# Two weight sums of a projection group on GpSimd, a fourth raw weight buffer there, and stores of x spread over an FFN's start

## The chip, the core and the metric

The kernel runs on one core of a Trainium2 chip. Five engines work side by side on their own queues: TensorE (PE; its weight loads are listed as PEld), VectorE (DVE), ScalarE (ACT), GpSimd (POOL) and SyncE (SP, which here only issues DMAs). Data lies in SBUF (128 partitions); matmul results lie in PSUM banks. The metric is the device time of one execution in microseconds. The kernel before takes 2344.84 us, the median of 3 runs (2342.85 to 2346.62).

## The reference

Two layers of an encoder trunk on 512 tokens of width 1024, all in float32. Each layer is: a half-step SwiGLU FFN, a mixer, a second half-step FFN, each with an RMSNorm before and after.

```python
for l in range(DEPTH):
    y = swiglu(rmsnorm(h, ffn1_pre_g[l]), ffn1_w_gu[l], ffn1_w_down[l])
    h = h + 0.5 * rmsnorm(y, ffn1_post_g[l])
    u = rmsnorm(h, mix_pre_g[l])
    proj = u @ w_in[l]
    qa, ka, va, qb, kb, vb, qc, kc, vc, gl = jnp.split(proj, split_at, axis=-1)
    ...  # neighbourhood, sliding-window and differential attention, gates, w_out
    h = h + rmsnorm(merged @ w_out[l], mix_post_g[l])
    y = swiglu(rmsnorm(h, ffn2_pre_g[l]), ffn2_w_gu[l], ffn2_w_down[l])
    h = h + 0.5 * rmsnorm(y, ffn2_post_g[l])
```

The change lies in `proj = u @ w_in[l]` of both layers and in the start of the first FFN.

## The kernel before

**Precision.** TensorE multiplies in a reduced float32 form. Every operand is therefore split into a high part (a rounding copy by ScalarE) and a low part (the raw value minus the high part, by DVE), and a product is three matmuls: high x high, high x low, low x high.

**Seven products.** Most of `w_in` and of the FFN's gate and up weights goes through `class Seven`: two column blocks of weights by the two halves of the inner dimension, times four quadrants of the activations, are computed as seven products in place of eight (a Strassen-like scheme). One such pair of column blocks is a *group*: 84 matmuls of 256 columns, line 687. A group needs two raw weight tiles of 128x1024 (512 KB each), which hold four 128x512 quarters, and sums of these quarters. For group g:

- `fetches` (L614) issues the two raw loads from SP's queue, into a pool `wr` of three buffers that rotate.
- `sum13` (L628, DVE, 128x1024) makes two sums into a tile r; `high1`, `low1` (L632, L637) split the first raw tile; `high13`, `low13` (L642, L647) split r.
- `sum2` (L651, DVE, 128x512) adds half of r and a quarter of the first raw tile into the second raw tile, in place.
- `high12`, `low12` (L657, L661) split a quarter of the second raw tile; `sum4` (L665, DVE, 128x512) then overwrites that quarter with its sum with the other one; `high24`, `low24` (L669, L674) split the whole second raw tile.

The four weight sums of a group are thus the two in `sum13`, `sum2` and `sum4`. The first raw tile is free after `low1` and `sum2`, the second after `low24`.

The products p1 to p7 of a group run while the weights of the next are prepared. ScalarE copies between banks (L726, L731, L735), DVE adds (`add21` L740, `add22` L745), and when `add22` is done a bank is free for a later group's first product.

**The projection** (`project`) has 13 groups a layer. What a group yields is evicted by ScalarE (L1396, L1400), split again (L1412, L1413), for queries and keys rotated (L1459 to L1461) or, for values, transposed by TensorE (L1434) and evicted (L1440, L1441), and stored to DRAM for the mixer: `store` (L1407) issues these DMAs from GpSimd's queue. The tiles for all this come from 16 buffers of the tag `t` (128x512 each). Beside its DMAs, GpSimd computes almost nothing in the kernel: some fills at the start and one-element copies (`mark`, L287) that pace DMAs in the FFNs.

**The order** of the instructions on each engine is not as written: a scheduler of the building layer sorts them, and each engine then executes its list strictly in order, each instruction waiting for its semaphores. A pool decides at build time which buffer a tile gets.

**The first FFN's start.** x comes in transposed; `keep` (L906 to L911) transposes it back, by TensorE into the one bank `o` (L908), copies it by ScalarE into a tile `h` (L910; from four buffers of the tag `t` that `finish` also uses, L853 to L856) and stores it to DRAM in two halves per token block, from SP's queue (L911). There are four token blocks, eight copies and eight stores of 256 KB. They stand in a list `later`, from which two entries are taken at each weight tile of the dense products that come before the first group.

Of the kernel before, what the change touches and what calls it, by code (L numbers as in the profile page):

```python
# [10 lines left out]
F32 = mybir.dt.float32  # L11
F32R = mybir.dt.float32r
AF = mybir.ActivationFunctionType
ALU = mybir.AluOpType
AX = mybir.AxisListType

P = 128
# [4 lines left out]
NT = T // P  # L22
FF = 2816
KF = FF // P
# [4 lines left out]
WB = 8  # L29
# [85 lines left out]
def encoder_kernel(ctx: ExitStack, tc: tile.TileContext, order, xT, wts, cols, rows, rpb, consts, tables, out):  # L115
# [9 lines left out]
    BUFS = {"X": 6, "n": 2, "wr": 3, "wp": 2, "wq": 2}  # L125
    WP = BUFS["wp"] + BUFS["wq"]
    SKEW = 80
    ABUFS = {"f": {"t": 4, "x": 10}, "p": {"t": 16, "x": 10, "rr": 2}, "m": {"t": 5, "h": 4, "rr": 2, "tx": 5, "st": 14, "gd": 2, "g": 10, "s": 2, "pt": 4}}
    PBUFS = {"mm": 2, "mx": 2, "at": 3, "o": 1}

    def open_phase(kind):
# [10 lines left out]
    def nm(s):  # L142
        serial[0] += 1
        return f"{s}{serial[0]}"
# [53 lines left out]
    def holder(tag):  # L198
        return lambda: [big(tag, F32R, (P, HB, P), name="w") for _ in range(2)]

    def fetch(parts, eng=None):
        raw = sb.tile([P, WB, P], F32, tag="wr", name=nm("wr"), bufs=BUFS["wr"])
        src = wts[len(stream["raw"])].rearrange("p (a b) -> p a b", b=P)
        for c in range(0, WB, WB // parts):
            cs = slice(c, c + WB // parts)
            (eng or stream["eng"]).dma_start(raw[:, cs, :], src[:, cs, :])
        stream["raw"].append(raw)
# [167 lines left out]
    class Squares:  # L375
        def __init__(self):
            self.acc, self.seen = None, []
# [203 lines left out]
    class Seven:  # L581


        def __init__(self, z, count):
            self.z, self.count = z, count
            self.hi, self.lo, self.raw = {}, {}, {}
            self.raws, self.W = {}, {}
            self.groups = [{} for _ in range(count)]
            self.seeds = None
# [24 lines left out]
        def fetches(self, g):  # L614
            if g < self.count:
                self.W[g] = {}
                for _ in range(2):
                    fetch(1, nc.sync)
                self.raws[g] = [t.rearrange("p (a b) c -> p a b c", a=2) for t in stream["raw"][-2:]]

        def wpair(self, name):
# [26 lines left out]

        def sum2(self, g):
            r = self.raws[g]  # L650
            V.tensor_tensor(out=r[1][:, 1], in0=self.W[g]["r13"][:, 1], in1=r[0][:, 0], op=ALU.add)  # L651

        def high12(self, g):
            w = self.W[g]
# [7 lines left out]

        def sum4(self, g):
            r = self.raws[g][1]
            V.tensor_tensor(out=r[:, 0], in0=r[:, 0], in1=r[:, 1], op=ALU.add)  # L665

        def high24(self, g):
            self.W[g]["h24"] = self.wpair("h24")
# [96 lines left out]
    def ffn(l, which, X, accs):  # L765
# [93 lines left out]
                V.scalar_tensor_tensor(out=place(m), in0=pu, scalar=-1.0, in1=t, op0=ALU.mult, op1=ALU.mult)  # L859


        S = Seven(z, KF - plain)
        hi, lo, raw, groups, count = S.hi, S.lo, S.raw, S.groups, S.count
        divide, less, quadrants = S.divide, S.less, S.quadrants
        later = stream["later"]
# [4 lines left out]
        def at(fn, *args):  # L870
            return lambda: fn(*args)
# [13 lines left out]
        if first:  # L885
            s = Squares()
            for hs in HALVES:
                for b in range(KD):
                    s.add(V, hT[:, b, hs], hs)
            rB = pair("rB", F32)[:, 0, :]  # L890
            u1 = dense1(gu, l, KF + 1, X.blocks, tag="at", midway=lambda: finish_rms(s, rB))
            prepare(rowt)
            n = [sb.tile([P, 2, HK, HT], F32, tag="n", name=nm("n"), bufs=BUFS["n"]) for _ in range(2)]
            own = [sb.tile([P, 2, HK, HT], F32R, tag="X", name=nm("X"), bufs=BUFS["X"]) for _ in range(2)]
            quadrants(n)

            def normal(b):
                V.scalar_tensor_tensor(
                    out=n[b // HK][:, :, b % HK, :], in0=two(hT[:, b, :]), scalar=gcol(b), in1=two(rB),
                    op0=ALU.mult, op1=ALU.mult,  # L900
                )

            def keep(tb):
                d = dr.tile([P, D], F32, tag="kept", name=nm("kept"), bufs=2 * NT)
                for i in range(2):
                    tp = bank("o")  # L906
                    for k in range(HB):
                        PE.transpose(tp[:, k * P : (k + 1) * P], hT[:, HB * i + k, tb * P : (tb + 1) * P], ident)  # L908
                    t = big("t", name="h")
                    A.activation(t, tp, AF.Copy)  # L910
                    nc.sync.dma_start(d[:, i * T : (i + 1) * T], t)  # L911
                kept.append(d)

            stream["pace"] = 2
            for b in range(0, KD, 2):
                later.append(some(at(normal, b), at(normal, b + 1)))
            later.append(at(divide, "11", own[0][:, 0], own[1][:, 0]))
            later.append(at(divide, "22", own[0][:, 1], own[1][:, 1]))
            later.extend(at(keep, tb) for tb in range(NT))
            later.append(at(gap, "gaph", 48))  # L920
        else:
            quadrants(X.raw)
            for i, j in ((0, 0), (1, 0), (1, 1)):
                k = f"{i + 1}{j + 1}"
                hi[k], lo[k] = X.hi[i][:, j], X.lo[i][:, j]
# [11 lines left out]
                at(S.low1, 0),  # L937
            )
        )
        if not first:  # L940
            u1 = dense1(gu, l, KF + 1, X.blocks, tag="at")
        finish(0, g0, u0)
# [427 lines left out]
    def project(l, op, accs):  # L1370
# [115 lines left out]
            now()  # L1486

        made = {}
        S = Seven(z, len(GROUPS))
        count, groups, later = S.count, S.groups, stream["later"]  # L1490

        def some(*calls):
# [2 lines left out]
        def at(fn, *args):  # L1495
            return lambda: fn(*args)
# [661 lines left out]
```

## Time and profile before

| what | us |
|---|---|
| median of 3 runs | 2344.84 (2342.85 to 2346.62) |
| profiled execution, its own time | 2345.54 |
| its span, first to last instruction | 2343.7 |
| PE busy | 2329.0 (99%) |
| DVE busy | 1917.7 (82%) |
| ACT busy | 1455.2 (62%) |
| POOL busy | 235.7 (10%) |
| mean granted TensorE clock | 0.999 of full speed |

Rows of a timeline give the start in us from the span's start, the duration in us, the engine, the source line, the operation, `out<-in` by the program's names and the shapes; in square brackets stands the engine's idle time before the instruction, and what ended it. Rows of groups give the busy time, the mean duration in ns, and the idle time before. A duration is longer than the distance to the next instruction's start where an engine overlaps the end of one with the start of the next, so that distance (the pitch) is what an instruction costs on a full engine.

### The profile page before, as it was taken

The numbers are of one execution on the slowest core, as the hardware profiler recorded it, in microseconds if no ns is written. First come the engines' busy times: TensorE is split into PE (matmuls) and PEld (weight loads), VectorE is DVE, ScalarE is ACT, GpSimd is POOL, SyncE is SP. The second block draws the span as 40 slices with busy tenths as digits, with TensorE's granted clock in tenths as the row PEclk, the third lists the DMA queues.
The fourth block names the chain that finished last, engine by engine and source line by source line (L and its number), as shares of the span: only waits on it lengthen the run. The fifth ranks groups of instructions, "written<-read, shape, count | busy, mean of one in ns | idle before, by whom it ended". The sixth has DMA issues, their size and how long they took to land.

```text
span 2343.7 us, 40580 instructions
## 1 busy us (share of the span) xinstructions
PE 2329.0 (99%) x15278; PEld 2104.4 (90%) x15278; DVE 1917.7 (82%) x3103; ACT 1455.2 (62%) x2734; POOL 235.7 (10%) x378
## 2 busy tenths in 40 slices
PE   9999999999999999999999999999999999999998
PEld 7999889998888889998899998899988888999987
DVE  8987988868987778888888878798689776888796
ACT  6565566668766465655665555666687764656563
POOL 0111001110122001110001100011102110011100
PEclk9999999999999999999999999999999999999999
DMA  5566446668556425665536565276775664356642
GB/s 190 148 172 194 147 150 194 200 218 241 150 179 214 149 96 151 168 160 161 171 103 165 166 171 197 92 219 197 231 221 147 187 207 142 97 162 171 180 142 92
DMA packets 135636, 395.18 MB, mean 169 GB/s; under 512 B 19216, under 2 KB 23952, under 8 KB 134928
## 3 DMA queue, kind: packets, MB, share of 16 engines
q1 hardware_dynamic: 99712, 260.11, 35.8%
q0 software_dynamic: 22080, 84.95, 13.3%
q10 hardware_dynamic: 13648, 47.53, 6.6%
q8 instruction: 120, 1.97, 0.4%
q14 instruction: 76, 0.62, 0.1%
HBM read 326.98 MB, written 80.74 MB: 174 GB/s over the span
## 4 chain that ended last, share of the span: by engine, by line
PE 88%; DMA 4%; DVE 3%; issue 2%; ACT 1%; SPq 0%; POOL 0%; ACTq 0%; DVEq 0%; POOLq 0%
PE mm L687 20%; PE mx L687 10%; PE mm L1155 8%; PE mm L323 6%; PE mm L322 6%; PE mm L324 6%; PE mx L1155 5%; PE at L687 5%; PE at L1155 5%; DMA wr<-in_wts_dram 2%; PE at L322 2%; PE at L323 2%; PE at L324 2%; PE o L1155 1%; PE mx L1677 1%
## 5 line engine op out<-in xcount | busy, mean ns | idle before, releaser
L687 PE MATMUL mm<-X,h 128*128 128x256 f32 x1600 | 285.5, 278 | 2.3 <-DVE v L745 2.2
L687 PEld LDWEIGHTS mm<-X,h 128*128 128x128 f32 x1600 | 243.1, 188 | 4.3 <-DVE v L745 3.4
L687 PE MATMUL mm<-ht,h 128*128 128x256 f32 x800 | 224.0, 280 | 1.0 <-ACT at L726 1.0
L687 PE MATMUL mm<-ht,l 128*128 128x256 f32 x800 | 223.6, 279 | 0.0
L687 PE MATMUL mm<-lt,h 128*128 128x256 f32 x800 | 222.8, 278 | 0.0
L687 PE MATMUL mx<-ht,h 128*128 128x256 f32 x800 | 221.6, 277 | 0.4 <-ACT v L731 0.2
L687 PE MATMUL mm<-X,l 128*128 128x256 f32 x800 | 221.5, 277 | 0.0
L687 PE MATMUL mx<-ht,l 128*128 128x256 f32 x800 | 221.2, 276 | 0.0
L687 PE MATMUL mx<-lt,h 128*128 128x256 f32 x800 | 221.2, 276 | 0.0
L219 ACT ACTIVATE w<-wr 128x512 fp32r<-128x512 f32 x240 | 148.1, 626 | 96.4 <-PE mm L324 54.7
L220 DVE TENSOR_TENSOR w<-wr,w 128x512 fp32r<-128x512 f32 x240 | 163.0, 687 | 49.6 <-ACT w L219 48.6
L322 PE MATMUL mm<-X,w 128*128 128x512 f32 (+1 forms) x516 | 196.3, 380 | 0.3 <-ACT w L219 0.3
L323 PE MATMUL mm<-X,w 128*128 128x512 f32 (+1 forms) x516 | 195.4, 379 | 0.2
L324 PE MATMUL mm<-X,w 128*128 128x512 f32 (+1 forms) x516 | 193.6, 375 | 0.0
L637 DVE TENSOR_TENSOR l<-wr,h 128x1024 fp32r<-128x1024 f32 x100 | 122.4, 1224 | 67.8 <-PE mm L687 67.6
L669 ACT ACTIVATE h<-wr 128x1024 fp32r<-128x1024 f32 x100 | 106.2, 1062 | 84.1 <-PE mx L687 56.1
L687 PE MATMUL at<-X,w 128*128 128x256 f32 x1200 | 153.7, 277 | 0.0
L687 PEld LDWEIGHTS mm<-ht,h 128*128 128x128 f32 x800 | 150.7, 188 | 1.6 <-ACT at L726 1.4
L687 PEld LDWEIGHTS mx<-ht,h 128*128 128x128 f32 x800 | 150.3, 188 | 1.1 <-ACT v L731 1.0
L687 PEld LDWEIGHTS mm<-ht,l 128*128 128x128 f32 x800 | 150.8, 188 | 0.3 <-DVE l L674 0.2
L687 PEld LDWEIGHTS mm<-lt,h 128*128 128x128 f32 x800 | 150.7, 188 | 0.0
L687 PEld LDWEIGHTS mx<-lt,h 128*128 128x128 f32 x800 | 150.3, 188 | 0.0
(462 smaller groups left out, 6767.0 us busy)
## 6 DMA issues: line engine op xcount, KB each, us to landing
wr<-in_wts_dram SPq DMA_DIRECT2D x284, 512.0 KB, 3.7
wr<-in_wts_dram ACTq DMA_DIRECT2D x90, 512.0 KB, 4.2
sum<-in_wts_dram POOLq DMA_DIRECT2D x64, 512.0 KB, 5.1
st<-part SPq DMA_DIRECT2D x120, 128.0 KB, 4.2
ap<-in_wts_dram SPq DMA_DIRECT2D x20, 512.0 KB, 6.0
a<-kept SPq DMA_DIRECT2D x32, 256.0 KB, 6.3
ap<-sum SPq DMA_DIRECT2D x16, 512.0 KB, 3.3
x<-part SPq DMA_DIRECT2D x32, 256.0 KB, 3.6
```

The lines of the kernel that those rows point to most:

```text
L219: A.activation(hi, raw, AF.Copy)
L220: V.tensor_tensor(out=lo, in0=raw, in1=f(hi), op=ALU.subtract)
L322: PE.matmul(acc, w[0], x[0], start=start, stop=False)
L323: PE.matmul(acc, w[0], x[1], start=False, stop=False)
L324: PE.matmul(acc, w[1], x[0], start=False, stop=stop)
L637: V.tensor_tensor(out=w["l1"], in0=self.raws[g][0], in1=f(w["h1"]), op=ALU.subtract)
L669: A.activation(self.W[g]["h24"], self.raws[g][1], AF.Copy)
L687: PE.matmul(acc, ws[i], xs[j], start=start and k == m == 0, stop=stop and k == n - 1 and m == 2, skip_group_check=True,)
L1155: PE.matmul(acc, x[i], w[j], start=start and n == 0, stop=stop and n == 2, skip_group_check=True)
L1677: PE.matmul(shaped(sp, k), qs, k, start=m == 0, stop=m == 1)
```

## The change

Three edits. In the projection's groups, from the third (g = 2) on, `sum2` and `sum4` are issued on GpSimd in place of DVE: 22 instructions a layer. The FFNs' groups keep them on DVE. In the projection, the second raw tile of each odd group goes to a buffer of its own, `wx`, so that the three `wr` buffers serve the other three raw tiles of two groups; the 4 KB a partition for it are taken from the tag `t`, which goes from 16 to 14 buffers. In the first FFN, the four entries of `keep` are no longer four in a row in the list `later` but stand one by one between its next entries. In the changed file, line numbers from the edits on are 1 to 4 higher.

```diff
-    ABUFS = {... "p": {"t": 16, "x": 10, "rr": 2}, ...}
+    ABUFS = {... "p": {"t": 14, "x": 10, "rr": 2}, ...}
...
-    def fetch(parts, eng=None):
-        raw = sb.tile([P, WB, P], F32, tag="wr", name=nm("wr"), bufs=BUFS["wr"])
+    def fetch(parts, eng=None, raw=None):
+        if raw is None:
+            raw = sb.tile([P, WB, P], F32, tag="wr", name=nm("wr"), bufs=BUFS["wr"])
...
-        def __init__(self, z, count):
-            self.z, self.count = z, count
+        def __init__(self, z, count, adder):
+            self.z, self.count, self.adder = z, count, adder
...
-                for _ in range(2):
-                    fetch(1, nc.sync)
+                for i in range(2):
+                    own = phase[0][0] == "p" and i and g % 2
+                    fetch(1, nc.sync, self.z("wx", F32, (P, WB, P)) if own else None)
...
         def sum2(self, g):
             r = self.raws[g]
-            V.tensor_tensor(out=r[1][:, 1], in0=self.W[g]["r13"][:, 1], in1=r[0][:, 0], op=ALU.add)
+            (self.adder if g > 1 else V).tensor_tensor(out=r[1][:, 1], in0=self.W[g]["r13"][:, 1], in1=r[0][:, 0], op=ALU.add)
...
         def sum4(self, g):
             r = self.raws[g][1]
-            V.tensor_tensor(out=r[:, 0], in0=r[:, 0], in1=r[:, 1], op=ALU.add)
+            (self.adder if g > 1 else V).tensor_tensor(out=r[:, 0], in0=r[:, 0], in1=r[:, 1], op=ALU.add)
...
-        S = Seven(z, KF - plain)
+        S = Seven(z, KF - plain, V)
...
-            later.extend(at(keep, tb) for tb in range(NT))
...
+        if first:
+            for tb in range(NT):
+                later.insert(len(later) - 10 + tb, at(keep, tb))
...
-        S = Seven(z, len(GROUPS))
+        S = Seven(z, len(GROUPS), G)
```

The scheduler sorts the changed program anew. Three places show what moved; the names are those of the program with the numbers of their tiles.

GpSimd, layer 0, from the last stores before the third group on. Before:

```order
43 L1407 DMA part_4099<-v_4092 128x512
44 L1407 DMA part_4301<-hi_4297 128x512
45 L1407 DMA part_4303<-lo_4298 128x512
46 L1407 DMA part_4314<-hi_4310 128x512
47 L1407 DMA part_4316<-lo_4311 128x512
48 L1407 DMA part_4385<-hi_4381 128x512
```

Now:

```order
43 L1411 DMA part_4099<-v_4092 128x512
44 L653 ISA
45 L653 TENSOR_TENSOR wr_4224<-r_4263,wr_4222 128x512
46 L667 TENSOR_TENSOR wr_4224<-wr_4224 128x512
47 L1411 DMA part_4301<-hi_4297 128x512
48 L1411 DMA part_4303<-lo_4298 128x512
49 L1411 DMA part_4314<-hi_4310 128x512
50 L1411 DMA part_4316<-lo_4311 128x512
51 L653 TENSOR_TENSOR wx_4365<-r_4409,wr_4363 128x512
52 L1411 DMA part_4385<-hi_4381 128x512
```

The sums of the third group (L653 and L667 are `sum2` and `sum4`) stand ahead of the stores that were next, and each later group's sums stand between its stores. Row 44, which the building layer adds once in the program, reloads a library of GpSimd's.

DVE, layer 0, the preparation of the second group (w, l, r are its splits and sums) and the start of the third's. Before:

```order
425 L637 TENSOR_TENSOR l_4171<-wr_4128,h_4152 128x1024
426 L651 TENSOR_TENSOR wr_4130<-r_4155,wr_4128 128x512
427 L647 TENSOR_TENSOR l_4190<-r_4155,h_4169 128x1024
428 L740 TENSOR_TENSOR v_4173<-mx_4137,v_4173 128x256
429 L665 TENSOR_TENSOR wr_4130<-wr_4130 128x512
430 L745 TENSOR_TENSOR v_4173<-mm_4136,v_4173 128x256
431 L1750 TENSOR_TENSOR edges_5100<-pre_5095 128x256 x2
432 L1750 TENSOR_TENSOR edges_5100<-pre_5095 128x128
433 L674 TENSOR_TENSOR l_4258<-wr_4130,h_4238 128x1024
434 L628 TENSOR_TENSOR r_4263<-wr_4224,wr_4222 128x1024
```

Now:

```order
424 L639 TENSOR_TENSOR l_4171<-wr_4128,h_4152 128x1024
425 L653 TENSOR_TENSOR wx_4130<-r_4155,wr_4128 128x512
426 L649 TENSOR_TENSOR l_4190<-r_4155,h_4169 128x1024
427 L742 TENSOR_TENSOR v_4173<-mx_4137,v_4173 128x256
428 L667 TENSOR_TENSOR wx_4130<-wx_4130 128x512
429 L1465 TENSOR_TENSOR x_4047<-x_4047,sh_4049 128x512
430 L747 TENSOR_TENSOR v_4173<-mm_4136,v_4173 128x256
431 L630 TENSOR_TENSOR r_4263<-wr_4224,wr_4222 128x1024
432 L676 TENSOR_TENSOR l_4258<-wx_4130,h_4238 128x1024
```

The second raw tile of this odd group is `wx_4130`, and the first sum of the next group (L630, `sum13`) now stands ahead of this group's last split (L676, `low24`).

ScalarE, first FFN: the copies of `keep` (h) among the roundings of weights (w), of activations (X, ht) and the finish (t). Before:

```order
54 L910 ACTIVATE h_446<-o_441 128x512
55 L219 ACTIVATE w_495<-wr_493 128x512
56 L910 ACTIVATE h_454<-o_449 128x512
57 L600 ACTIVATE X_359<-n_358 128x1024
58 L910 ACTIVATE h_463<-o_458 128x512
59 L219 ACTIVATE w_544<-wr_493 128x512
60 L910 ACTIVATE h_471<-o_466 128x512
61 L206 DMA wr_611<-in_wts_dram 128x1024
62 L854 ACTIVATE t_486<-t_486 128x512
63 L910 ACTIVATE h_504<-o_499 128x512
```

Now:

```order
54 L912 ACTIVATE h_447<-o_442 128x512
55 L220 ACTIVATE w_479<-wr_477 128x512
56 L912 ACTIVATE h_455<-o_450 128x512
57 L601 ACTIVATE X_359<-n_358 128x1024
58 L220 ACTIVATE w_512<-wr_477 128x512
59 L207 DMA wr_611<-in_wts_dram 128x1024
60 L856 ACTIVATE t_470<-t_470 128x512
61 L912 ACTIVATE h_489<-o_484 128x512
62 L220 ACTIVATE w_551<-wr_549 128x512
63 L601 ACTIVATE ht_515<-n_358 128x1024
```

Before, four copies came ahead of the finish of the third block (t_486); now two do (ahead of t_470).

More of the change, by code (lines that the diff above doesn't have):

```diff
@@ L127, in encoder_kernel @@
     SKEW = 80
-    ABUFS = {"f": {"t": 4, "x": 10}, "p": {"t": 16, "x": 10, "rr": 2}, "m": {"t": 5, "h": 4, "rr": 2, "tx": 5, "st": 14, "gd": 2, "g": 10, "s": 2, "pt": 4}}
+    ABUFS = {"f": {"t": 4, "x": 10}, "p": {"t": 14, "x": 10, "rr": 2}, "m": {"t": 5, "h": 4, "rr": 2, "tx": 5, "st": 14, "gd": 2, "g": 10, "s": 2, "pt": 4}}
     PBUFS = {"mm": 2, "mx": 2, "at": 3, "o": 1}
```

## The prediction

> **What bounds the kernel now.** I read the page's busy times first, then who makes TensorE wait, then the projection window by window.
>
> ```profile
> span 2343.7 us, 40580 instructions
> PE 2329.0 (99%) x15278; PEld 2104.4 (90%) x15278; DVE 1917.7 (82%) x3103; ACT 1455.2 (62%) x2734; POOL 235.7 (10%) x378
> ```
>
> TensorE is busy 99% of the span, so the change can only win back the few places where it stands still. The waits, for PE alone, name them:
>
> ```profile
> PE mm L687 <- DVE v L745: 2.2, 5, 1.0
> PE o L908 <- ACT h L910: 1.6, 1, 1.6
> PE mm L687 <- ACT at L726: 1.0, 1, 1.0
> PE at L1434 <- DVE v L1441: 0.8, 1, 0.8
> ```
>
> L687 is the product of every seven-product group, L908 the transposes that keep x, L1434 the transposes of the values. The second row belongs to the first FFN, the others to the two projections. How much time the projections lose shows when their groups stand beside an FFN group of the same 84 matmuls (columns: window, its length, then busy time of PE, PEld, DVE, ACT, POOL, the clock, the DMA share, GB/s):
>
> ```profile
> 1557.25:1650.94 93.69, 91.73 (x779) 90.15 (x777) 83.78 (x117) 59.19 (x114) 17.82 (x34) 1.00 0.65 206
> 396.28:498.23 101.95, 100.22 (x862) 99.13 (x861) 90.94 (x128) 65.71 (x125) 19.89 (x38) 1.00 0.66 210
> 103.29:112.89 9.60, 9.60 (x86) 9.60 (x85) 7.97 (x11) 5.42 (x9) 1.47 (x3) 1.00 0.57 167
> ...
> 396.28:406.24 9.96, 9.96 (x90) 9.96 (x89) 9.39 (x15) 7.71 (x18) 2.84 (x7) 1.00 0.83 266
> 406.24:417.26 11.02, 10.50 (x92) 10.27 (x90) 10.49 (x18) 6.42 (x16) 2.08 (x4) 1.00 0.64 195
> ```
>
> The last row but one is a group with one set of four transposes and no stall: 9.96 - 9.60 = 0.36 us for the set. The long window of layer 0 holds ten groups and five sets: 10 x 9.60 + 5 x 0.36 = 97.8 us of work in 101.95, so 4.15 us are lost. That of layer 1 holds nine groups and five sets: 86.4 + 1.8 = 88.2 in 93.69, 5.5 us lost. **9.65 us is all that the projections can give**, and the keep of x adds 1.6. In these windows DVE is 89% busy: it is the engine that comes next.
>
> Why does TensorE wait there? One stall of each kind, DVE at 410 us and ScalarE at 1635 us:
>
> ```profile
> 409.65 0.42 DVE L1441 TENSOR_TENSOR v<-at,v 128x256 fp32r<-128x256 f32 x1
> 410.60 1.23 DVE L628 TENSOR_TENSOR r<-wr,wr 128x1024 f32<-128x1024 f32 x1 [0.53 <-DMA wr<-in_wts_dram]
> 411.74 0.42 DVE L1441 TENSOR_TENSOR v<-at,v 128x256 fp32r<-128x256 f32 x1
> 412.07 0.42 DVE L745 TENSOR_TENSOR v<-mm,v 128x256 f32<-128x256 f32 x1
> ...
> 1635.01 0.64 ACT L657 ACTIVATE w<-wr 128x512 fp32r<-128x512 f32 x1 [2.47 <-DMA wr<-in_wts_dram]
> 1635.55 1.04 ACT L632 ACTIVATE h<-wr 128x1024 fp32r<-128x1024 f32 x1
> 1636.49 0.37 ACT L726 ACTIVATE at<-mm 128x256 f32<-128x256 f32 x1
> ```
>
> The first weight sum (L628) waits for its raw tile; behind it on DVE stands L745, which empties the bank that TensorE wants. On ScalarE the copy L726, for which TensorE waits, stands behind a rounding that waits for the same load. So these stalls begin with **a raw weight tile that lands late**, because with three buffers its load is issued only when the group before has let one go. In layer 0's window the wait adds up to the idle time in the first row here:
>
> ```profile
> L628 DVE TENSOR_TENSOR r<-wr,wr 128x1024 f32<-128x1024 f32 x10 | 12.2, 1224 | 4.8 <-DMA wr<-in_wts_dram 4.8
> L665 DVE TENSOR_TENSOR wr<-wr 128x512 f32<-128x512 f32 x11 | 7.6, 687 | 0.1
> L651 DVE TENSOR_TENSOR wr<-r,wr 128x512 f32<-128x512 f32 x10 | 6.8, 684 | 0.0
> L740 DVE TENSOR_TENSOR v<-mx,v 128x256 f32<-128x256 f32 x10 | 4.2, 421 | 0.9 <-PE mx L687 0.9
> L745 DVE TENSOR_TENSOR v<-mm,v 128x256 f32<-128x256 f32 x10 | 4.2, 419 | 0.0
> L1441 DVE TENSOR_TENSOR v<-at,v 128x256 fp32r<-128x256 f32 x6 | 2.5, 420 | 0.0
> ```
>
> **The fourth raw buffer.** On the queue the second tile of every odd group goes to a buffer of its own; the three old ones then serve three tiles in two groups, so each load may start about a group's length (9.6 us) after its buffer fell free instead of right at it. The waits quoted are 0.5 to 2.5 us, and a load takes 3.7, so they should go:
>
> ```profile
> wr<-in_wts_dram SPq DMA_DIRECT2D x284, 512.0 KB, 3.7
> ```
>
> I count the stalls that start with a load as half of the 9.65 us: **-5 us**; from 0 (if the queue, not the buffer, delays them) to -7. The two stores' buffers that pay for it (16 to 14) I put at nothing: the tiles that live in them are mostly freed within two groups, and the adds ahead of a store in GpSimd's queue delay it by a microsecond or two. Were they short, TensorE's evictions would wait and each shortage cost about 1 us.
>
> **The sums on GpSimd.** DVE loses 21 instructions in layer 0's window (L651 and L665). Their pitch is below their duration:
>
> ```profile
> 402.97 0.69 DVE L651 TENSOR_TENSOR wr<-r,wr 128x512 f32<-128x512 f32 x1
> 403.57 0.69 DVE L661 TENSOR_TENSOR w<-wr,w 128x512 fp32r<-128x512 f32 x1
> ```
>
> 0.60 us each, 12.6 together; DVE's 90.94 falls to 78.3. Were that all, DVE would have 19 us of air. But before shows no add on GpSimd. Nearest rows are its fills, its stores' issues, and the one-element marks:
>
> ```profile
> L1407 POOL DMA_DIRECT2D part<-hi x30 | 16.3, 544 | 452.8 <-ACT hi L1412 419.3 <-ACT v L735 32.6 <-issue 0.3
> L292 POOL MEMSET ones<- 128x128 f32 x1 | 0.2, 204 | 0.3 <-POOLq L2108 0.3
> L293 POOL MEMSET eps<- 128x1 f32 x1 | 0.1, 98 | 0.0
> ...
> 93.88 1.03 POOL L287 COPY mark<-a 128x1 f32<-128x1 f32 x1 [8.12 <-DVE a L982]
> 1009.65 0.76 POOL L287 COPY mark<-a 128x1 f32<-128x1 f32 x1 [8.42 <-DVE a L982]
> ...
> 93.66 1.22 DVE L647 TENSOR_TENSOR l<-r,h 128x1024 fp32r<-128x1024 f32 x1
> 1009.15 1.22 DVE L647 TENSOR_TENSOR l<-r,h 128x1024 fp32r<-128x1024 f32 x1
> ```
>
> A fill costs (204 - 98)/127 = 0.83 ns an element. An add of 512 reads two streams: one after the other, 2 x 512 x 0.83 + 98 = 0.95 us; with the write in turn too, 1.37. DVE's 0.69 is the lower bound. I take 1.15, between the upper two. The marks tell more: a copy of one element takes 1.03 us, and ends at 94.91, just behind DVE's L647 (93.66 + 1.22 = 94.88); when it starts later it takes 0.76 and ends at 1010.41, again just behind L647's end at 1010.37. **GpSimd stands still until a DVE instruction that reads two SBUF tiles is over.** That DVE waits for GpSimd in turn no row shows, since a mark is too short to stop anything. If it does, adds and DVE instructions take turns: 78.3 + 21 x 1.15 = 102.5 us, less where an add runs beside one of the 26 instructions that read PSUM (L740, L745, L1441), at most 26 x 0.33 = 8.6 (the pitch from 411.74 to 412.07). Between 93.9 and 102.5; the middle, 98.2, against TensorE's 97.8: 0.4 a layer, **+0.8 us**, from -4.6 (no turns, DVE never late: the rest of the 9.65) to +10.3 (1.37 us each, no overlap: 107.1 against 101.95, twice).
>
> The waits that this adds: GpSimd's queue holds a sum that waits for DVE's r tile, and behind it the stores of the projection's parts. A sum delayed by 1 us delays these by 1 us. The rounding L669 on ScalarE, then L674 on DVE, wait for the second sum; in the new order the next group's first sum stands ahead of L674 on DVE and covers 1.14 us of it (its pitch, 410.60 to 411.74).
>
> GpSimd's list has one more new row, an ISA instruction ahead of its first sum. No row of before prices it. What hides it is GpSimd's idle time after its store at 384.69:
>
> ```profile
> 384.69 0.54 POOL L1407 DMA_DIRECT2D part<-v  x1 [1.53 <-DVE v L1441]
> 395.81 0.54 POOL L1407 DMA_DIRECT2D part<-hi  x1 [10.58 <-ACT v L735]
> ```
>
> That is about 10 us until the first sum is wanted; above it, each microsecond goes to TensorE, once. I take 0.
>
> The Trainium skill, GPSIMD Engine Reference, section Instruction dispatch, has about 6 us for the first call after a kernel library is loaded. By it the sum stays as it is.
>
> **The stores that keep x.** Their PE wait above, 1.6 us, comes from ScalarE's copy, which waits for a store to give back one of four buffers:
>
> ```profile
> 49.53 0.60 ACT L910 ACTIVATE h<-o 128x512 f32<-128x512 f32 x1 [2.78 <-DMA kept<-h]
> ...
> 43.79 5.64 DMA kept<-h
> 50.84 0.23 PE mm L322
> ```
>
> (The last two rows are of the chain of waits.) A store there took 5.64 us. In the new order the third copy wants the first one's buffer still about 2 us after its store is issued, so it may wait; but 21 matmuls of 0.23 us, 4.8 us, stand between its transposes and the next ones on TensorE, which hide that. The fifth and sixth copies take buffers that the finish (L853 to L856) frees, the seventh one whose store is some 8 us old. I take **-1.6 us**, from 0 to -1.6. Cover: DVE's chain for the first group ends with TensorE's own last dense product, so it comes earlier with it.
>
> **The sum.** The profiled execution took 2345.5 us (span 2343.7 and 1.8 around it): 2345.5 - 5 + 0.8 - 1.6 = 2339.7. It lies 0.7 above the median 2344.84 of the runs, so I forecast **2339**, 2336 to 2343 for this case.
>
> **The rivals.** (1) *GpSimd's adds never hold DVE up.* For it: nothing in before shows DVE waiting for GpSimd. Against it: the marks. DVE then has air, and 8 of 9.65 us go: 2344.8 - 8 - 1.6 = 2335. (2) *Slower: the adds hold the read path that DVE's second input needs.* For it: the marks show that path as one that only one engine has at a time. It decides where 78.3 + 21p exceeds 101.95, at p = 1.13 us without overlap. At 1.37 that is 5.2 us a window, 10.3 in all, 8.7 after the keep: 2353.5; with half of the greatest overlap (4.3 us a window) 2345. I price it between, 2350: earlier loads help nothing when DVE itself sets the pace, and L745 is late at every group. (3) *The loads are late for another reason,* the queue ahead of them or the DMA share of 0.65, and DVE's air is spent in turns: only the keep is won, 2343.5.
>
> The Trainium skill, SBUF — State Buffer, section Who interferes with whom, states rival 2's rule for both directions: a DVE instruction with two SBUF inputs and a GpSimd instruction that reads SBUF exclude each other for the whole of the one that starts first. The trace agrees for GpSimd waiting (94.91 against 94.88); no run here yet shows the reverse.
>
> **How the numbers follow.** Forecast 0.42, rival 1 0.19, rival 2 0.26, rival 3 0.13. 0.2% is 4.7 us, about what a measurement of this kernel can tell from no change; the border is 2340.2. Of the forecast's 0.42, 0.29 lie below it and 0.13 above; rival 1 is faster; rival 2 gives 0.23 slower and 0.03 same; rival 3 same 0.13. Faster 0.48, same 0.29, slower 0.23. The range leaves out the ends of rivals 1 and 2: 2334.5 to 2351.5.
>
> **What would show it.** Right: in the projections no idle time before L628 that ends with a raw load; group windows near 9.6 and 9.96 us; no PE wait for L908's copy near 50 us. The adds' spans tell of the turns: 1.0 to 1.4 us where they start with DVE idle or on PSUM, and longer beside L637, L647 or L674. Rival 2 shows as DVE instructions with two SBUF inputs well above 1.22 us and a window above 102; rival 1 as adds and unstretched DVE instructions at the same time. A gap of over 10 us at GpSimd's first sum would make the ISA row the cause. I am wrong if DVE's idle time for loads stays, or if ScalarE's L669 waits more than 1 us a group for GpSimd and TensorE behind it.

## The result and the profile after

The changed kernel takes **2373.36 us** (median of 4 runs, 2370.37 to 2374.84), the kernel before 2345.73 in the same comparison. The ratio is 1.0122, with a 95% interval of 1.011 to 1.0134: 27.6 us slower. The forecast was 2339, faster. The profiled execution took 2370.37. Of the ten runs of one kernel further down (three fills) two took 5992 and 13297 us; its ratio leaves these two out.

The page's first rows of the changed kernel (busy time, share of the span, instructions):

```profile
span 2368.6 us, 40652 instructions
PE 2336.1 (99%) x15278; PEld 2111.0 (89%) x15278; DVE 1915.9 (81%) x3059; ACT 1459.0 (62%) x2734; POOL 311.2 (13%) x422
```

DVE has 44 instructions fewer than before, and its busy time is the same: 1915.9 against 1917.7 us. 44 sums at the pitch of 0.60 us are 26 us, so something else has filled them. The waits of TensorE in the changed kernel (us in total, times, longest):

```profile
PE mm L689 <- DVE v L747: 13.4, 8, 2.9
PE at L1438 <- DVE lo L1417: 5.6, 2, 4.0
PE at L1438 <- DVE v L1445: 3.4, 2, 1.9
...
PE mx L1681 <- DMA st<-part: 1.3, 2, 0.9
```

The row of L908, the copy that keeps x, is gone. The first three rows, those of the projections, come to 22.4 us; the prediction had listed 2.2 + 1.0 + 0.8 = 4.0 for the kernel before. The same windows as before, ten groups of layer 0 and nine of layer 1 (window, length, busy PE, PEld, DVE, ACT, POOL, clock, DMA share, GB/s):

```profile
396.44:512.47 116.03, 103.56 (x863) 102.17 (x862) 91.49 (x110) 66.73 (x124) 53.42 (x57) 0.97 0.56 183
1571.93:1675.28 103.35, 93.76 (x779) 92.79 (x777) 85.52 (x101) 59.63 (x112) 50.75 (x54) 0.97 0.57 187
```

They were 101.95 and 93.69 us long: 14.08 and 9.66 us more, 23.7 of the 24.9 us by which the span grew. So the loss lies in the projections: DVE carries the same load in a longer time, and the granted clock has fallen from 1.00 to 0.97.

**What happens to one add.** Three lines of the changed kernel in the views by source line (shortest, median and longest duration in ns):

```profile
L649 DVE TENSOR_TENSOR l<-r,h x100: 1209/1220/2323, 65.4 to 2233.8; 128x1024 fp32r<-128x1024 f32 x100
...
L747 DVE TENSOR_TENSOR v<-mm,v x100: 407/418/425, 77.5 to 2245.8; 128x256 f32<-128x256 f32 x100
...
L653 POOL TENSOR_TENSOR wx<-r,wr x10: 1287/2192/2208, 400.9 to 1662.2; 128x512 f32<-128x512 f32 x10
```

The low part L649 reads two SBUF tiles; its longest takes 1.1 us more than the median. L747 reads one operand from PSUM and never stretches. An add takes 1.29 us where nothing disturbs it, and mostly 2.2 where something does (3.95 at most). The timeline shows the turn-taking, and what comes of it (start, duration):

```profile
441.34 1.23 DVE L630 TENSOR_TENSOR r<-wx,wr 128x1024 f32<-128x1024 f32 x1 [4.80 <-DMA wx<-in_wts_dram]
442.48 1.22 DVE L639 TENSOR_TENSOR l<-wr,h 128x1024 fp32r<-128x1024 f32 x1
442.65 2.21 POOL L653 TENSOR_TENSOR wx<-r,wr 128x512 f32<-128x512 f32 x1 [5.00 <-DVE r L630]
443.62 2.32 DVE L649 TENSOR_TENSOR l<-r,h 128x1024 fp32r<-128x1024 f32 x1
...
448.15 1.57 POOL L667 TENSOR_TENSOR wx<-wx 128x512 f32<-128x512 f32 x1 [3.30 <-DVE w L663]
448.53 1.75 DVE L1464 TENSOR_TENSOR sh<-sh,sinR 128x512 f32<-128x512 f32 x1
450.20 0.41 DVE L747 TENSOR_TENSOR v<-mm,v 128x256 f32<-128x256 f32 x1
...
450.67 0.58 PE L689 MATMUL mm<-X,h 128*128 128x256 f32 x1 [2.92 <-DVE v L747]
```

The add issued at 442.65 stands still while L639 runs (to 443.70) and reads until 444.86. L649, issued at 443.62, stands still in turn and ends at 445.94, 1.08 us after the add, where it would have needed 1.22. At 448.15 the second add does the same to L1464. DVE executes in order, so L747 comes late by both, and by the 4.80 us that L630 waited for its raw tile; TensorE, which needs the bank that L747 empties, stands still for 2.92 us.

### The profile page after: what moved, and what is told of

Its sections match the earlier page's. It is cut to its first block, busy times and chain, and to the rows that moved or that the text cites. A ratio compares the mean times of both kernels' runs of the same rounds, so it can differ in the third digit from the quotient of the medians.

```text
span 2368.6 us, 40652 instructions
## 1 busy us (share of the span) xinstructions
PE 2336.1 (99%) x15278; PEld 2111.0 (89%) x15278; DVE 1915.9 (81%) x3059; ACT 1459.0 (62%) x2734; POOL 311.2 (13%) x422
## 3 DMA queue, kind: packets, MB, share of 16 engines
q0 software_dynamic: 22080, 84.95, 13.1%
## 5 line engine op out<-in xcount | busy, mean ns | idle before, releaser
L639 DVE TENSOR_TENSOR l<-wr,h 128x1024 fp32r<-128x1024 f32 x100 | 124.9, 1249 | 72.0 <-PE mm L689 72.0
L689 PEld LDWEIGHTS mm<-X,l 128*128 128x128 f32 x800 | 152.3, 190 | 0.0
```

Source lines behind the costliest of these rows:

```text
L639: V.tensor_tensor(out=w["l1"], in0=self.raws[g][0], in1=f(w["h1"]), op=ALU.subtract)
L689: PE.matmul(acc, ws[i], xs[j], start=start and k == m == 0, stop=stop and k == n - 1 and m == 2, skip_group_check=True,)
```

## The experiments

Medians and ratios to the kernel before, each from its own comparison. Line numbers shift by a few between the kernels.

| kernel | sums | raw buffers, t | us | ratio, 95% interval |
|---|---|---|---|---|
| the change | both on GpSimd | 4, 14 | 2373.36 | 1.0122 (1.011 to 1.0134) |
| spread stores alone | DVE | 3, 16 | 2344.18 | 0.9999 (0.9989 to 1.0008) |
| fourth buffer | DVE | 4, 14 | 2347.75 | 1.0014 (1.0005 to 1.0024) |
| both sums | both on GpSimd | 3, 16 | 2359.42 | 1.0064 (1.0049 to 1.0079) |
| adds that nobody needs | DVE, 44 adds more | 3, 15 | 2378.80 | 1.015 (1.0133 to 1.0167) |
| sum2 alone | sum2 on GpSimd | 4, 14 | 2366.19 | 1.0089 (1.0074 to 1.0104) |
| sum4 alone | sum4 on GpSimd | 4, 14 | 2362.36 | 1.0069 (1.0054 to 1.0084) |
| buffers given out anew | DVE | 4, 14 | 2345.61 | 1.0004 (0.9994 to 1.0013) |
| the same, with both sums | both on GpSimd | 4, 14 | 2364.25 | 1.0079 (1.0062 to 1.0096) |
| single fills | filled, not summed | 3, 16 | 2341.20 | 0.9985 (0.9976 to 0.9994) |
| three fills | filled, not summed | 3, 16 | 2347.09 | 1.0011 (1.0001 to 1.0021) |
| the change, three fills | filled, not summed | 4, 14 | 2347.31 | 1.001 (1.0 to 1.0019) |
| copies that nobody needs | DVE, 44 copies more | 3, 15 | 2354.31 | 1.0038 (1.0024 to 1.0053) |

All but the two with work that nobody needs have the spread stores.

### The parts alone

The spread stores alone:

```diff
-        S = Seven(z, len(GROUPS), G)
+        S = Seven(z, len(GROUPS), V)
...
-                    fetch(1, nc.sync, self.z("wx", F32, (P, WB, P)) if own else None)
+                    fetch(1, nc.sync, self.z("wx", F32, (P, WB, P)) if False else None)
...
-    "p": {"t": 14, ...}
+    "p": {"t": 16, ...}
```

> Only the spread stores of x; the sums stay on DVE, no fourth buffer, 16 buffers of tag t. Both theories: the 1.6 us wait at 50 us goes and nothing else moves, ratio 0.9993, 1.5 to 2 us faster. If it were slower, the spread stores themselves would have a part in the loss of 27.6 us.

2344.18 us, 0.7 below the kernel before in the same comparison. That can be told neither from nothing nor from the 1.6 us that were expected; the wait itself is gone, as the head of TensorE's list of waits shows:

```profile
PE at L539 <- DVE a L491: 2.1, 1, 2.1
PE mm L689 <- DVE v L747: 1.6, 3, 0.7
```

The fourth buffer with the sums on DVE (the first line of the diff above alone):

> Spread stores and the fourth raw buffer (t 14), the sums on DVE. Theory A (the adds on GpSimd carry the loss: DVE stands still while one reads SBUF, and what waits for an add comes later): no loss here, about 2340 to 2343 us, and little or no idle time of DVE behind a load of wx. Theory B (the fourth buffer carries it: it is freed only when the second low part of its group is made, its next load stands at the head of SP's queue until then, and every load behind it is late): DVE still waits about 10 us a layer for wx, 2355 to 2370 us.

2347.75: 3.6 us slower than the spread stores alone, so the buffer does not help. (The scheduler also put the instructions of TensorE, DVE and ScalarE into another order here, so the 3.6 us are those of the buffers together with that order.) SyncE's waits in layer 0's projection, first in the kernel before, then here:

```profile
SPq L206 <- DVE l L674: 30.1, 8, 6.8
SPq L206 <- DVE l L637: 26.5, 5, 7.4
SPq L206 <- DVE wr L651: 15.9, 4, 6.5
```

```profile
SPq L207 <- DVE l L639: 44.3, 8, 7.6
SPq L207 <- DVE l L676: 27.8, 8, 6.1
...
SPq L207 <- DVE wx L653: 2.6, 1, 2.6
...
DVE r L630 <- DMA wx<-in_wts_dram: 7.0, 3, 3.9
```

With three rotating buffers, the first raw tile of a group takes the buffer that the second low part (L674) of two groups before lets go, and the second one that which `sum2` of the group before lets go. The four buffers take away the wait for `sum2` (15.9 to 2.6 us) and leave the other: now the second tile waits for the second low part of two groups before (27.8 us, eight times, as before). The first sum needs both tiles.

Both sums on GpSimd with three buffers (the other two pieces of the diff above):

> Spread stores and the two sums on GpSimd, but three raw buffers and 16 of tag t as before. Theory A: about 2365 to 2375 us, the stretched DVE instructions as in the changed kernel (about 13 us a layer). Theory B: no wx, so no loss: 2340 to 2347 us.

2359.42. The adds alone cost 15.2 us on the spread stores (2344.18), the buffer alone 3.6, both together 29.2: 10.4 us come only of the two together, in the order that the scheduler gives them. Theory B is out as the whole of the cause, theory A does not explain what the buffer adds.

### Does an add hold DVE, whoever needs it?

The kernel before, with this called behind `sum13` and behind `sum4`:

```diff
+        def beside(self, g):
+            if phase[0][0] == "p" and g > 1:
+                t, r = self.z("sc", F32, (P, HB, P)), self.W[g]["r13"]
+                G.tensor_tensor(out=t, in0=r[:, 1], in1=r[:, 0], op=ALU.add)
```

> The kernel before, with 22 adds a layer on GpSimd more, from r into a tile that nobody reads (128x512, one buffer of tag t fewer); PE, DVE, ACT and SP keep their order. No result depends on them, so only what an add does to the other engines by running is measured. If a GpSimd add holds DVE's two-input instructions still: DVE's busy time in a projection rises by some 13 us (14 of 22 adds at 1.1 us, less where one falls on a PSUM instruction), and with DVE then at 119 of 123 us the time rises by 5 to 25 us. If the adds do not hold DVE: DVE's durations stay, and the time within 2 us of before.

**2378.80, 33.9 us slower**, more than expected. Its page and one place of its timeline:

```profile
PE 2338.5 (98%) x15278; PEld 2110.7 (89%) x15278; DVE 1959.7 (82%) x3103; ACT 1455.9 (61%) x2734; POOL 310.3 (13%) x422
...
440.75 0.42 DVE L753 TENSOR_TENSOR v<-mm,v 128x256 f32<-128x256 f32 x1
440.98 1.29 POOL L635 TENSOR_TENSOR sc<-r 128x512 f32<-128x512 f32 x1 [2.76 <-DVE r L628]
441.08 1.74 DVE L658 TENSOR_TENSOR wr<-r,wr 128x512 f32<-128x512 f32 x1
```

The same instructions of DVE are busy 42.0 us longer (1959.7 - 1917.7): 0.95 us for each of the 44 adds. L658, 0.68 us by itself, starts 0.10 us after the add and ends 0.55 us behind the add's end. L753, which reads PSUM, runs at its 0.42, and ScalarE's busy time is what it was (1455.9 against 1455.2). No result waits for these adds, so the loss is that of the hold, but for some 3 us: at the mixer's start TensorE waits 3.2 us for stores that stand behind the adds in GpSimd's queue, 0.2 before.

### What is it about the add?

In place of each sum, fills of the same tile, one or three in a row (these kernels leave out two weight sums of four, so their products are not those of the reference):

```diff
         def sum2(self, g):
-            (self.adder if g > 1 else V).tensor_tensor(out=r[1][:, 1], in0=self.W[g]["r13"][:, 1], in1=r[0][:, 0], op=ALU.add)
+            if g > 1 and self.adder is G:
+                for _ in range(3):
+                    G.memset(r[1][:, 1], 0.0)
+                return
+            V.tensor_tensor(out=r[1][:, 1], in0=self.W[g]["r13"][:, 1], in1=r[0][:, 0], op=ALU.add)
...
         def sum4(self, g):
-            (self.adder if g > 1 else V).tensor_tensor(out=r[:, 0], in0=r[:, 0], in1=r[:, 1], op=ALU.add)
+            if g > 1 and self.adder is G:
+                for _ in range(3):
+                    G.memset(r[:, 0], 0.0)
+                return
+            V.tensor_tensor(out=r[:, 0], in0=r[:, 0], in1=r[:, 1], op=ALU.add)
```

> Three raw buffers, 16 of tag t, spread stores, and on GpSimd, in place of each of the 44 sums, a fill with zeros of the same 128x512 tile (so two weight sums of four are left out): it writes SBUF, reads none, takes about 0.5 us and stands in the same place; DVE, PE, ACT and SP keep the order of the kernel with both sums on GpSimd and three buffers (2359.4 us). Theory H (the reads of the adds hold DVE, and that is the loss): no DVE instruction is stretched, DVE has 26 us of air, 2336 to 2344 us. Theory W (what hurts is that the result comes from another engine, over semaphores): 2352 to 2360 us. If writing SBUF holds DVE too: two-input instructions stretched by up to 0.5 us.

> As the last one, with three such fills in a row in place of each sum: about 1.6 us each, near the mean span of the adds there (1.82 and 1.60 us), still without a read of SBUF (the two sums are left out). Theory H: at most 3 us over the one with single fills. Theory L (an add's result comes 1 us later than DVE's, and the roundings, L676 and L747 behind it are late): most of the loss is back, 2352 to 2360 us.

> The changed kernel (fourth raw buffer, t 14), with three fills in a row on GpSimd in place of each sum (the two sums are left out). Theory H: 2340 to 2350 us, no stretched DVE instruction. Theory L, and the load of wx held back by a late L676: 2360 to 2373 us, with some 10 us a layer of DVE waiting for wx.

With single fills the kernel takes 2341.20, faster than before. PE, DVE, ACT and SP have the order of the kernel with both sums and three buffers: **adds in place of fills cost 18.2 us** (2359.42 - 2341.20). Page and source view of the kernel with single fills:

```profile
PE 2326.8 (99%) x15278; PEld 2103.0 (90%) x15278; DVE 1891.5 (81%) x3059; ACT 1457.4 (62%) x2734; POOL 259.9 (11%) x422
...
L649 DVE TENSOR_TENSOR l<-r,h x100: 1212/1219/1226, 63.2 to 2203.2; 128x1024 fp32r<-128x1024 f32 x100
```

No L649 is longer than 1.226 us: the fills, which only write SBUF, hold nothing here. DVE is relieved of the expected 26.2 us (1917.7 - 1891.5).

Three fills, about 1.7 us of GpSimd for each sum, come to 2347.09, 5.9 above single fills. Theory H allowed 3, theory L asked for 11 or more. DVE and ScalarE have another order in some places of this kernel, so the 5.9 us are not the fills' alone. Part of it is elsewhere: in the mixer TensorE waits for the projection's parts, whose stores stand behind the sums in GpSimd's queue. The rows of three fills and of a single one:

```profile
PE mx L1689 <- DMA st<-part: 5.1, 3, 3.1
```

```profile
PE mx L1689 <- DMA st<-part: 1.2, 2, 0.7
```

That is 3.9 of the 4.7 us between the two spans (2343.4 and 2338.7).

In the changed kernel itself, three fills for each sum give 2347.31, 2.1 us above the kernel before in the same comparison: **25.5 of its 27.6 us are gone with the reads**. PE, DVE, ACT and SP have the order of the change, and three fills keep GpSimd for 1.7 us, about as long as an add there (2.02 us in the mean for `sum2`, 1.42 for `sum4`). This kernel also settles the buffer's part. Page, and DVE's idle time before L630 until a raw tile is there, in both layers:

```profile
PE 2327.4 (99%) x15278; PEld 2103.4 (90%) x15278; DVE 1888.0 (81%) x3059; ACT 1456.7 (62%) x2734; POOL 304.8 (13%) x510
```

```profile
  DMA wx<-in_wts_dram: 20.6, 6
```

And the same row of the changed kernel:

```profile
  DMA wx<-in_wts_dram: 21.5, 6
```

DVE waits as long for wx as in the changed kernel, and it costs next to nothing, since DVE has 27.9 us of air (1915.9 - 1888.0). The late buffer is harmless where DVE has room and costs 13.9 us (2373.36 - 2359.42) where the holds have taken it.

### One sum alone

For sum2 alone `sum4` is issued on DVE again, for sum4 alone `sum2`:

```diff
-            (self.adder if g > 1 else V).tensor_tensor(out=r[:, 0], in0=r[:, 0], in1=r[:, 1], op=ALU.add)
+            V.tensor_tensor(out=r[:, 0], in0=r[:, 0], in1=r[:, 1], op=ALU.add)
```

> The changed kernel with sum4 back on DVE; sum2 alone on GpSimd, 22 adds in all. Base is the fourth buffer without adds, 2347.8 us; both adds cost 25.6 us on it. Theory P (each add costs by the time in which it holds DVE, whatever it computes): half, about 2360 us. Theory L (an add costs by what waits for its result: nothing is near behind sum2, since sum4 and the rounding L671 come later): DVE is stretched by about 13 us in both layers together all the same, but the time is about 2352 us.

> The changed kernel with sum2 back on DVE; sum4 alone on GpSimd, 22 adds. Theory P: about 2360 us, as with sum2 alone. Theory L: sum4 stands ahead of L671 on ScalarE, L676 on DVE and the load that waits for L676's buffer, so most of the loss is here, 2365 us or more, though its 22 adds stretch DVE no more than those of sum2.

2366.19 and 2362.36: 18.4 and 14.6 us above the 2347.75 of the fourth buffer without adds. Theory L is out as the whole cause: the sum for whose result nothing waits soon costs no less than the other. Theory P had 12 for each; both together cost 25.6, less than the 33.0 of the two apart. The cost of an add is not a fixed one.

DVE's busy time tells why the two differ. In the fourth-buffer kernel it is 1914.7 us; without 22 sums that would be some 1901.6 (half of the 26.2 us above taken off). It is 1920.2 with sum2 alone and 1911.5 with sum4 alone: an estimated 18.6 and 9.9 us of hold. The spans of these profiled executions (2365.2 and 2356.6, the latter of the fastest run of its kernel) lie 19.6 and 11.0 us above the 2345.6 of the fourth-buffer kernel. So sum2 costs more because it holds DVE for longer. A late result has a part too, in one place of sum4 alone:

```profile
455.80 7.43 POOL L667 TENSOR_TENSOR wr<-wr 128x512 f32<-128x512 f32 x1 [0.83 <-issue]
...
463.26 1.06 ACT L671 ACTIVATE h<-wr 128x1024 fp32r<-128x1024 f32 x1 [4.07 <-POOL wr L667]
```

DVE has eight instructions with two SBUF inputs in a row there, the last of which ends at 462.06; the add comes through behind them, and ScalarE waits 4.07 us for it.

### The buffers given out in another way

The first raw tile of every group in the buffer of its own, the second one in the three that rotate, and loaded first:

```diff
-                for i in range(2):
-                    own = phase[0][0] == "p" and i and g % 2
-                    fetch(1, nc.sync, self.z("wx", F32, (P, WB, P)) if own else None)
+                own = phase[0][0] == "p"
+                n = len(stream["raw"])
+                first = self.z("wx", F32, (P, WB, P)) if own else sb.tile([P, WB, P], F32, tag="wr", name=nm("wr"), bufs=BUFS["wr"])
+                both = [first, sb.tile([P, WB, P], F32, tag="wr", name=nm("wr"), bufs=BUFS["wr"])]
+                for i in (1, 0) if own else (0, 1):
+                    nc.sync.dma_start(both[i], wts[n + i].rearrange("p (a b) -> p a b", b=P))
+                stream["raw"].extend(both)
```

> The four raw buffers given out in another way, sums on DVE, t 14, spread stores: the first raw tile of every group, which is done with early, has the one buffer of its own, and the second, which lives until L676, has the three rotating ones and is loaded first. Then no load waits for the L676 of two groups before. If that wait is why the fourth buffer gained nothing: DVE's wait for loads at L630 falls from 9 us a layer to under 3 and the time to 2337 to 2343 us. If the loads are late for another reason, or the 14 buffers of tag t carry the 2.9 us: 2345 to 2349 us.

> The same way of giving out the buffers, with both sums on GpSimd. If the loss of the changed kernel beyond that of the adds with three buffers (2373.4 against 2359.4) comes from the load that waits for L676's late end: it goes, and the time is 2350 to 2360 us, with little wait for loads; what is left is the adds' own. If it comes from the adds' hold on DVE alone: 2368 to 2375 us as in the changed kernel.

With the sums on DVE the waits for raw tiles in layer 0's projection fall to this row, from 4.8 us before and 9.5 (7.0 for wx, 2.5 for wr) in the fourth-buffer kernel:

```profile
DVE r L634 <- DMA wx<-in_wts_dram: 1.8, 4, 0.8
```

The time is 2345.61, that of before. So earlier loads are to be had with four buffers, and they are **worth nothing that can be measured** here. With both sums on GpSimd this way of giving out the buffers takes 2364.25, 9.1 less than the change, so the late wx had its share; but 4.8 more than with three buffers, and above the 2350 to 2360 that were expected. Why it stays above the three buffers is open.

### Is one input enough?

The adds that nobody needs, as copies of one half of r:

```diff
-                G.tensor_tensor(out=t, in0=r[:, 1], in1=r[:, 0], op=ALU.add)
+                G.tensor_copy(out=t, in_=r[:, 1])
```

> The kernel before, with 44 copies on GpSimd more, from half of r into a tile that nobody reads (128x512, one SBUF input), in the places of the 44 adds that no result depended on; PE, DVE, ACT and SP keep their order. Those adds stretched 44 DVE instructions by 45.6 us and cost 33.9 us. If what holds DVE is any GpSimd read of SBUF: DVE is stretched by the copy's own length, an estimated 0.4 to 0.6 us each (a fill of this size takes 0.53), 17 to 26 us in all, and the time rises by 10 to 20 us. If it needs two inputs on GpSimd as it does on DVE: no DVE instruction is stretched, and the time is within 2 us of before.

2354.31, 9.7 us slower (the profiled execution is the longest of its runs, 2358.61). The copies and the page:

```profile
L635 POOL COPY sc<-r x44: 616/946/3825, 394.4 to 1667.7; 128x512 f32<-128x512 f32 x44
...
PE 2331.8 (99%) x15278; PEld 2105.4 (89%) x15278; DVE 1931.9 (82%) x3103; ACT 1456.3 (62%) x2734; POOL 281.0 (12%) x422
```

One SBUF input on GpSimd is enough to hold DVE: 14.2 us (1931.9 - 1917.7) for 44 copies of 0.62 us, just below the expected 17. One copy took 3.825 us: GpSimd can be kept out for several DVE instructions in a row, as the add of 7.43 us was.

## Why the prediction was wrong

**What bounds the kernel** was read right as far as it named DVE as the next engine in the projections, and wrong in the size of what was to be won. 9.65 us came from comparing group windows with one short group of each kind; the page's own waits summed to 4.0. The kernel with single fills shows that most of the difference was never a wait: with DVE relieved of 26 us, a transposing group of it still takes 10.43 us, with TensorE busy for 10.35, and the ten groups of layer 0 take 101.18.

```profile
475.13:485.56 10.43, 10.35 (x92) 10.15 (x90) 7.25 (x9) 6.59 (x12) 4.29 (x8) 1.00 0.61 215
393.98:495.16 101.18, 100.39 (x863) 99.22 (x861) 78.68 (x107) 66.59 (x126) 30.90 (x58) 1.00 0.66 211
```

The prediction called 97.8 us of the 101.95 work and the rest loss. Here DVE is busy 78.68 us, close to the 78.3 that it had reckoned without the sums, and the window is only 0.8 us shorter. Why these groups need more time than an FFN group's pace gives is open.

All of DVE's relief, without any hold, is worth 3.0 us (2344.18 - 2341.20).

**The fourth raw buffer, -5 us: wrong in sign and in mechanism.** The step that failed is "each load may start about a group's length after its buffer fell free". It counted tiles per buffer, and did not ask which instruction ends the life of each tile. The second tile lives until L676, so its load still waits for L676 of two groups before; by itself the buffer cost 3.6 us. That the late loads cost TensorE half of what was lost failed too: where they are gone (1.8 us), nothing is gained. How much of the 3.6 is due to the 14 buffers of tag t was not tried apart, nor is the other order; the kernel with the buffers given out anew has 14 as well, and stands 1.4 us above the spread stores alone, within the uncertainty.

**The sums on GpSimd, +0.8 us: the mechanism right, the size wrong by more than 14 us.** The price of an add, 1.15 us, was below but near the 1.29 measured, and both directions of the turn-taking are now shown, DVE's in the stretched L649 and in the adds that nobody needs. The bound that the prediction gave for 1.37 us and no overlap was +10.3; both sums with three buffers cost 15.2. The step that failed is the sum itself, 78.3 + 21 x 1.15 set against the length of the whole window. It takes DVE's time as something that can be moved about. In the changed kernel DVE is busy 91.49 us in its window, hardly more than the 90.94 of before: removed sums and added holds cancel. But what was removed was worth 3.0 us in all, while a hold falls on a two-input instruction wherever the add happens to start, and costs most of its length. In the profiled executions the span is longer by 26.1 us for 27.9 us of hold in the change (against its three-fill twin), by 18.8 for 26.6 with both sums and three buffers (DVE busy 1918.1 us, against single fills with 1891.5), by 33.3 for 42.0 with the adds that nobody needs, and by 13.1 for 14.2 with the copies. Of these, 0.9, 1.8, 3.0 and 3.5 us are longer waits at the mixer's start, for stores that stand behind GpSimd's work; the prediction had put the delay of the stores at nothing.

The Trainium skill, SBUF — State Buffer, section Who interferes with whom, was quoted for the reverse direction, which no run showed then. The runs agree with it in four points: DVE stands still for the add (L649, 2.32 us), an instruction with a PSUM operand does not (L747, 0.42), fills do not hold (1.226 at most), and a GpSimd read of one tensor is enough (14.2 us). It was given 0.26 as rival 2, and priced too low.

**The ISA row on GpSimd, 0 us: right.** The trace has two configuration instructions of 37 ns there; the first add follows the load of its raw tile, 6.8 us later, so a delay of up to that length would not show:

```profile
L653 POOLq MODIFY_POOL_CONFIG  x2: 37/37/37, 384.5 to 384.6; - x2
...
391.39 1.29 POOL L653 TENSOR_TENSOR wr<-r,wr 128x512 f32<-128x512 f32 x1 [6.86 <-DMA wr<-in_wts_dram]
```

**The stores that keep x, -1.6 us: right in mechanism**, the wait is gone in every kernel that has them. In the medians it shows as 0.7, which cannot be told from nothing.

**The rivals.** Rival 2 (2350) is what happened, with the marks that it was to leave in the trace: stretched two-input instructions and a window above 102 us. Its price lacked two things. It took no account of where the holds fall, and it held the buffer to be useless at worst, where the buffer multiplied the loss: 10.4 us come only of both edits together. Rival 1 (no hold, 2335) is refuted as a mechanism; even without a hold only 2341.2 is reached. Rival 3 had one thing right that the forecast had wrong: earlier loads win nothing.

The parts now add up. TensorE's waits in the projections grew by 18.4 us (4.0 to 22.4), those at the mixer's start by 1.1 (0.2 to 1.3), the keep fell by 1.6, and 6.5 us come from the clock (shown in the last section): 24.4 of the 24.9 us of span.

## What to carry to other kernels

Before work is moved from VectorE to GpSimd, count VectorE's instructions with two SBUF inputs near the place: a GpSimd add or copy that reads SBUF holds up the one that is issued while it runs, up to the add's or copy's own length, so the move pays only where its reads meet PSUM operands or an idle VectorE. A sum of busy times over a long window does not price this, since a hold can cost seven to nine tenths of its length while the time freed elsewhere is worth little; measure the hold by itself, with work that nobody needs. And a further buffer helps only the tile whose release comes last: ask for each tile which instruction ends its life, and whether an earlier load is worth anything; here it was not (2345.61).

## What the runs showed that was not expected

**A stall costs more than itself.** Behind some waits of 1.85 us and more, TensorE runs at half its clock for 3.41 us. Two waits of the changed kernel in the timeline:

```profile
1625.91 0.39 PE L689 MATMUL mm<-X,h 128*128 128x256 f32 x1 [2.40 <-DVE v L747]
...
1647.49 0.39 PE L689 MATMUL mm<-X,h 128*128 128x256 f32 x1 [1.88 <-DVE v L747]
```

And windows of 3.41 us around the wait of 2.92 us that ends at 450.67, around that of 2.40 and around that of 1.88 (the last number but two is the granted clock):

```profile
446.69:450.10 3.41, 1.05 (x10) 0.85 (x8) 3.41 (x4) 0.51 (x2) 1.57 (x1) 1.00 0.70 217
450.10:453.51 3.41, 2.84 (x13) 2.85 (x14) 3.03 (x7) 0.91 (x2) 0.00 (x0) 0.50 0.19 73
453.51:456.92 3.41, 3.41 (x32) 3.41 (x32) 3.41 (x4) 1.36 (x3) 0.00 (x0) 1.00 0.23 58
...
1620.87:1624.28 3.41, 2.64 (x24) 2.45 (x22) 3.41 (x6) 2.11 (x3) 0.88 (x1) 1.00 0.62 177
1624.28:1627.70 3.42, 1.79 (x15) 1.79 (x16) 3.38 (x6) 0.97 (x3) 0.70 (x1) 1.00 0.46 169
...
1644.76:1648.18 3.42, 1.54 (x13) 1.34 (x12) 3.27 (x5) 1.07 (x4) 1.10 (x3) 1.00 0.44 120
1648.18:1651.59 3.41, 3.41 (x19) 3.41 (x18) 1.23 (x2) 0.57 (x2) 1.27 (x1) 0.50 0.50 187
```

19 matmuls fill the slow window at 1648.18, 32 the fast one at 453.51. The length of a wait alone does not decide: that of 1.88 us has a slow stretch behind it, that of 2.40 has none. The place does. The trace has four slow stretches in the projections, from 450.10, 494.47, 1579.91 and 1648.18 us on. Each lasts 3.41 us, and the distances between their starts are 13, 318 and 20 times 3.413 us, so in this trace the clock changes on a grid of that step. In the step ahead of each of the four, TensorE stood still for 2.36, 2.55, 1.85 and 1.88 us. The wait of 2.40 us is cut by a border of the grid, and no step holds more than 1.63 us of standing still there (3.42 - 1.79). A sharp limit is not shown: with sum4 alone, a step with 1.87 us is followed by the full clock (486.04) and one with 1.84 by half of it (1615.85).

At half the clock half of the time is lost: 1.4 us of the first stretch, in which TensorE works from 450.67 on, and 1.7 of each other one make the 6.5 us above. The mean granted clock of the whole execution is 0.996 in the change, with the adds that nobody needs and with the buffers given out anew for both sums, 0.995 with sum2 alone, and 0.999 with single fills. That may be one reason why the cost of a hold is uneven: a short wait costs itself, some longer ones themselves and up to another 1.7 us. Whole executions do not show it plainly: of the four with the adds that nobody needs, the one with a mean clock of 0.996 took 2378.75 us and the one with 0.999 took 2377.55. The Trainium skill, TensorE: Matmul & The Clock Gate, section What's actually happening, has the clock halve after an idle window of about 3.4 us; here it halved after steps of 3.41 us in which TensorE had stood still for 1.85 to 2.55 us, so a step that is idle throughout was not needed.

**Holds in a dead end.** Adds on GpSimd for whose results no other engine waits cost 33.9 us, more than the change that they were to explain; three fills in place of each sum, which keep GpSimd about as long, leave the changed kernel 2.1 us from the one before.

**No version that was tried beats the kernel before and computes all the sums.** The spread stores alone, 0.9999 (0.9989 to 1.0008), are all of the change that is worth keeping, and that by their trace rather than by their time.
